# An encoder layer with unnormalised x tiles and the token norm applied at the projections' outputs

## The chip, the cores and the metric

The kernel runs on one core of a Trainium2 chip. The metric is the device time of one execution in microseconds, as the median of several runs. Engines are named as in the profile: PE (TensorE, with PEld for its weight loads), DVE (VectorE), ACT (ScalarE), POOL (GpSimd) and SP (the queue that issues nearly all DMAs).

## The reference

One hybrid encoder layer is applied to 768 tokens (512 of a prompt, 256 of a sample) of width 2048, in float32:

```
h = rms_norm(x, norm_g)                     # x / sqrt(mean(x^2)) * gain, a factor for each token
proj = h @ w_in                             # 2048 x 8224
attn = dilated_attention(aq, ak, av) * silu(ag)        # 8 heads x 128, three windows merged
q, k, v = silu(short_conv(dq, dk, dv))                 # centred, 5 taps, each channel for itself
dn = rms_norm(delta_rule_fwd + delta_rule_bwd) * silu(dg)   # gated DeltaNet, 8 heads, two directions
y = rms_norm(x + concat(attn, dn) @ w_out, final_gain)
```

The norm of the input is a factor for each token (over x's 2048 channels) times a gain for each channel. The projections are linear, so the token's factor may stand before or behind them.

## The kernel before, in words

Activations lie with channels on partitions: x comes as 16 tiles of 128 channels by 768 tokens. Every projection gives a tile of 128 output channels by 768 tokens in two PSUM banks (512 and 256 columns). Float32 accuracy comes from splitting each operand into a rounded high part and a rest (`w_split` L319, `x_split` L425) and adding three products: high by high, high by low, low by high (`kstep` L335). A high part is a cast on ScalarE, a low part a subtraction on VectorE (on GpSimd in some single tiles).

An order for all engines is written out while the program is built. A `Driver` (L68) runs the TensorE program as the main line and a clock of costs for each engine; between matmuls it takes up to three steps of side tasks, smallest priority number first. A task that yields `AHEAD` (2.0) goes on 2 us before its own work is expected to end. Each engine and each DMA queue then runs its instructions in the order in which they were written out.

The stages, in order:

1. As x tiles land, `arrivals` (L433) makes their split parts with the channel gain but without the token factor, and sums squares. The first call of `project_two` (L588, called at L1588) projects two DeltaNet gates from them, two output tiles at a time, and the 32 columns of decay and beta inputs; `raw_gate_post` (L881) multiplies their outputs by rB, the token factor on all partitions, which `start_rms` (L909) has by about 58 us.
2. A second `project_two` (L1592) does two more gates in the same way. Beside it `norm` (L748) goes through the 16 tiles as soon as the second projection has used each: VectorE multiplies the x tile by gain and rB in place, ScalarE casts the new high part over the old one, VectorE subtracts for the low part. For eight of the tiles the right halves are stored to DRAM (bD, L763), because they are overwritten later.
3. A third `project_two` (L1593, "std") makes q and k of attention head 0 from the normalised parts; it waits for each tile.
4. Ten pairs of weight tiles (v, gates of attention, last gates) are projected by a seven-product scheme for 2 x 2 blocks instead of eight (`pair_products` L662, table `PRODUCTS` L64): each pair in two halves (input tiles 0 to 7 and 8 to 15), each half seven products of 12 matmuls of 384 columns in banks X, Y and Z. `evacuate` (L695) combines the banks. The right operands T1 to T4 are sums of quarters of x. `block_sums` (L767) makes them, once for all pairs: eight calls, each with four differences (T1f, T2f, T3f, T4f) and four split results. T2's parts are written over the right half of an x tile's parts, once the third projection has used it (`reached["std"] > a`, L781). T3's two subtractions run on GpSimd, the other six on VectorE. `normalise` (L814) runs the norm and then the eight sums, one after the other. `restore` (L822) brings the right halves back from bD after the last pair.
5. 24 convolution tiles and the rest of attention's q and k, one tile at a time (`project` L632). `conv_post` (L833) copies a tile out of PSUM into the buffer cin and adds five taps: for q and k on VectorE, for v (tile 16 and on) with a ScalarE multiply into ctmp and a GpSimd add. DeltaNet's work (`prep`, `merge`, `chain`, `head_out`) and later attention (`scores`, `attend`) run as side tasks. Attention's heads alternate between two sets of buffers (`SETS`, L1408), whose V is loaded into cin or ctmp.
6. The output projection in two parts (DeltaNet's channels, then attention's), L1756 to L1798, beside the end of attention; then the final norm.

Of the kernel before, what the change touches and what calls it, by code (L numbers as in the profile page):

```python
# [6 lines left out]
F32 = mybir.dt.float32  # L7
# [250 lines left out]
def encoder_kernel(tc, x, xT, wt, wab, wo, convw, gain, dngain, fgain, alog, dtb, cst, tabs, y):  # L258
# [43 lines left out]
    with (  # L302
# [59 lines left out]
        set_pool(ap, dict({f"t{i}": (3 * KB, 1) for i in range(24)}, f768=(3 * KB, 3), half=(HALF, 3), rB=(T, 1), m=(5 * P, 1)))  # L362
        sums3 = [ap.tile([P, HALF], F32, name=f"sum{i}") for i in range(3)]

        if True:
# [51 lines left out]
            rB = st("rB", (T,), "rB")  # L417
# [277 lines left out]
            def evacuate(x, pr):  # L695
# [42 lines left out]
                if pr in (2, 3, 7, 4):  # L738
                    yield 0
                    x["n"][side] += 1  # L740
                    if ph and x["n"][side] == 2:
                        kind, h = x["kind"][side]
                        spawn(put_out(kind, h, x["out"][side]), -4)


            normal = set()

            def norm():  # L748

                for k in range(NK + 1):  # L750
                    if k < NK:
                        yield from wait(lambda: reached["raw"] > k)
                        xn = xstage[k]
                        V.scalar_tensor_tensor(out=xn, in0=xn, scalar=g_in[:, k:k + 1], in1=rB, op0=ALU.mult, op1=ALU.mult)
                        xtiles(k, "n")
                        A.copy(xh[k], xn)
                    if k:
                        p = k - 1
                        V.tensor_tensor(out=xl[p], in0=xstage[p], in1=xh[p].bitcast(F32), op=ALU.subtract)
                        normal.add(p)  # L760
                        if p % 8 < 4:

                            for t, d in zip((xh[p], xl[p]), bD[4 * (p // 8) + p % 4]):  # L763
                                SY.dma_start(d, t[:, HALF:].bitcast(F32))
                    yield AHEAD

            def block_sums(ph, i):  # L767
# [4 lines left out]
                t, d = {}, {}  # L772

# [22 lines left out]
                yield from diff("T3", xb[:, hi], xa[:, hi], G)  # L796
# [9 lines left out]
                low("T3", G)  # L806
# [7 lines left out]
            def normalise():  # L814
                yield from wait(lambda: "rms" in flags)
                yield from norm()
# [16 lines left out]
            def conv_post(ctile, dst, room, done):  # L833

                def conv(acc):
# [5 lines left out]
                    for j in range(1, 5):  # L841
                        if ctile >= 16:
                            ctmp = Z["ctmp"]
                            A.mul(ctmp, cin[:, j:j + w], cw[:, j:j + 1])
                            G.tensor_tensor(out=acc, in0=acc, in1=ctmp, op=ALU.add)
                            yield "early"
                        else:
                            V.scalar_tensor_tensor(out=acc, in0=cin[:, j:j + w], scalar=cw[:, j:j + 1], in1=acc,
                                                   op0=ALU.mult, op1=ALU.add)
                            yield "bulk"  # L850
# [10 lines left out]
                def post(ps):  # L861
                    yield from get("cin", "cacc")
                    for h in (0, 1):
                        o = (2, TP + 6)[h]
                        A.copy(Z["cin"][:, o:o + width[h]], ps[h][:, :width[h]])
# [5 lines left out]
            def spill_post(kind, h):  # L871

                def post(ps):
                    yield from get("f768")
                    t = f768(f"{kind}{h}")
                    A.copy(t[:, parts[0]], ps[0][:, :TP])
                    V.tensor_copy(t[:, parts[1]], ps[1][:, :TS])
# [133 lines left out]
            def conv_tiles():  # L1011
                Z["cin"] = st("cin", (T + 8,), "cin")
                Z["ctmp"] = st("ctmp", (T + 4,), "ctmp")
# [370 lines left out]
            def halves(h, what):  # L1384
# [16 lines left out]
                else:  # L1401
# [7 lines left out]
                    dict(vT="ctmp", V=("oacc", "DN"), tab="PB", g="PBT", s=("D0", "X0")))  # L1409
# [91 lines left out]
            def put_out(kind, h, t):  # L1501

                if kind in "gd":
# [335 lines left out]
```

## Time and profile before

| | |
|---|---|
| median of 3 runs (lowest to highest) | 1695.9 us (1695.44 to 1698.59) |
| the profiled execution: time, span | 1694.39 us, 1692.7 us |
| busy, share of the span | PE 94%, PEld 83%, DVE 53%, ACT 50%, POOL 19% |
| mean granted TensorE clock | 0.98 |
| PE's busy tenths in 40 slices of 42.3 us | 7994999999999999999999999999999889897995 |
| DVE's | 6689777767545453455435355544346545433332 |

A slice's digit is its busy share in tenths, 9 for 90% or more. A group of instructions is a line with its operation, the tile it writes and those it reads (buffer numbers left out); as most instructions go through one helper, L204 or L286 stands for nearly all, and the tile's name tells them apart: xst is an x tile, xh_n and xl_n its normalised parts, raw, hip and lop weight parts, st a loaded weight quarter, S its sums, mmr, mm, mmX, mmY, mmZ PSUM banks, sum and out what `evacuate` writes, cacc the convolution's sum, av and V attention's V, T1f a difference and T1s its split result. A wait is the idle time of an engine ahead of an instruction, and the row names what ended it.

### The profile page before, as it was taken

How to read it: one execution, taken by the hardware profiler on the slowest of the kernel's cores; microseconds unless marked ns; L12 is line 12 of the kernel's file. 1: busy time of each engine (PE TensorE's matmuls, PEld its weight loads, DVE VectorE, ACT ScalarE, POOL GpSimd, SP SyncE). 2: the span in 40 equal slices, each digit the busy share in tenths (PEclk: the TensorE clock that was granted, in tenths of full speed). 3: DMA queues.
4: the chain of work that ended last, by engine and by line, in shares of the span. 5: the costliest groups of instructions: out<-in, count | busy, mean ns of one | idle time of the engine just before them, and what ended most of it. 6: DMA issues, size and time to landing. Idle time of an engine off the chain costs nothing. (4 is left out here: it accounts for less than half of the span.)

```text
span 1692.7 us, 30222 instructions
## 1 busy us (share of the span) xinstructions
PE 1599.3 (94%) x11675; PEld 1411.9 (83%) x11675; DVE 896.6 (53%) x1903; ACT 852.2 (50%) x1896; POOL 316.2 (19%) x281
## 2 busy tenths in 40 slices
PE   7994999999999999999999999999999889897995
PEld 6884999999988898888898888888887777775774
DVE  6689777767545453455435355544346545433332
ACT  6554333343456665656575655665365444432322
POOL 0003000000125231424132323332100111101220
PEclk9997999999999999999999999999999999998998
DMA  6241232232523222232223122223344554346457
GB/s 241 86 139 44 79 108 94 94 108 93 199 75 94 70 82 82 79 103 77 80 75 106 61 79 79 90 74 100 107 158 161 179 178 157 113 138 214 151 170 273
DMA packets 135263, 198.50 MB, mean 117 GB/s; under 512 B 49392, under 2 KB 60240, under 8 KB 135120
## 3 DMA queue, kind: packets, MB, share of 16 engines
q1 hardware_dynamic: 133968, 193.43, 35.3%
q10 hardware_dynamic: 1152, 3.15, 0.5%
q8 instruction: 92, 1.51, 0.4%
q14 instruction: 51, 0.42, 0.1%
HBM read 150.08 MB, written 46.45 MB: 116 GB/s over the span
## 5 line engine op out<-in xcount | busy, mean ns | idle before, releaser
L286 PE MATMUL mm<-xh_n,lop 128*128 128x512 f32 (+1 forms) x1152 | 306.4, 347 | 0.0
L286 PE MATMUL mm<-xl_n,hip 128*128 128x512 f32 (+1 forms) x1152 | 306.0, 347 | 0.0
L286 PE MATMUL mm<-xh_n,hip 128*128 128x512 f32 (+1 forms) x1152 | 304.3, 345 | 0.0
L204 ACT CAST hip<-st 128x512 fp32r<-128x512 f32 x244 | 150.8, 619 | 228.1 <-PE mm L286 90.5
L204 DVE TENSOR_TENSOR lop<-st,hip 128x512 fp32r<-128x512 f32 x172 | 126.2, 734 | 236.0 <-ACT hip L204 214.4
L204 POOL TENSOR_TENSOR lop<-st,hip 128x512 fp32r<-128x512 f32 x72 | 96.6, 1342 | 620.2 <-ACT hip L204 571.2
L286 PEld LDWEIGHTS mm<-xh_n,hip 128*128 128x128 f32 x1152 | 176.2, 189 | 22.4
L286 PEld LDWEIGHTS mm<-xl_n,hip 128*128 128x128 f32 x1152 | 176.5, 189 | 21.6
L286 PEld LDWEIGHTS mm<-xh_n,lop 128*128 128x128 f32 x1152 | 176.4, 189 | 21.6
L204 ACT ACTIVATE s<-s,m 128x512 f32<-128x512 f32 (+1 forms) x96 | 61.9, 649 | 103.6 <-DVE m L204 103.3
L286 PE MATMUL mmo<-oh,xh_m 128*128 128x512 f32 x192 | 80.4, 419 | 8.6 <-ACT oh L204 6.8
L286 PE MATMUL mmo<-oh,mh 128*128 128x512 f32 x192 | 76.9, 400 | 11.7 <-ACT mh L204 10.9
L286 PE MATMUL mmo<-ol,xh_m 128*128 128x512 f32 x192 | 78.2, 407 | 3.2 <-POOL ol L204 2.2
L204 POOL TENSOR_TENSOR cacc<-cacc,ctmp 128x772 f32<-128x772 f32 x32 | 59.1, 1846 | 116.6 <-ACT ctmp L204 116.5
L204 DVE SCALAR_TENSOR_TENSOR cacc<-cin,cw,cacc 128x772 f32<-128x772 f32 x64 | 71.0, 1109 | 18.4 <-ACT cacc L204 17.5
L286 PE MATMUL mmo<-ol,mh 128*128 128x512 f32 x192 | 76.7, 400 | 0.5 <-DVE ol L204 0.5
L286 PE MATMUL mmo<-oh,xl_m 128*128 128x512 f32 x192 | 77.0, 401 | 0.0
L286 PE MATMUL mmo<-oh,ml 128*128 128x512 f32 x192 | 76.4, 398 | 0.0
L286 PE MATMUL mmX<-xh_n,hip 128*128 128x384 f32 x160 | 54.3, 340 | 18.5 <-ACT sum L204 18.0
L286 PE MATMUL mmr<-xh_x,raw 128*128 128x512 f32 (+1 forms) x256 | 60.1, 346 | 10.5 <-ACT xh_x L204 10.5
L204 ACT ACTIVATE z<-c,rho 128x128 f32<-128x128 f32 x96 | 35.1, 366 | 65.0 <-PE c L286 64.8
L204 DVE TENSOR_TENSOR ol<-st,oh 128x512 fp32r<-128x512 f32 x52 | 42.2, 843 | 36.5 <-ACT oh L204 36.4
(267 smaller groups left out, 3495.2 us busy)
## 6 DMA issues: line engine op xcount, KB each, us to landing
st<-in_wt SPq DMA_DIRECT2D x256, 256.0 KB
st<-in_wo SPq DMA_DIRECT2D x64, 256.0 KB
dec<-gcD SPq DMA_DIRECT2D x24, 256.0 KB
res<-in_x SPq DMA_DIRECT2D x24, 256.0 KB
yD<-res SPq DMA_DIRECT2D x24, 256.0 KB
res<-yD SPq DMA_DIRECT2D x24, 256.0 KB
out_y<-row SPq DMA_DIRECT2D x12, 512.0 KB
xst<-in_xT SPq DMA_DIRECT2D x15, 384.0 KB
```

The costliest lines, as they stand in the source:

```text
L204: r = f(*a, **k)
L286: r = PE.matmul(out, lhsT, rhs, start=start, stop=stop, skip_group_check=more)
```

## The change

The token factor is not multiplied into x any more. `norm` is gone; the split parts of the first projections serve all later ones. Where a projected tile leaves PSUM, it is multiplied by rB: in `conv_post` and `spill_post` in place of a copy (on VectorE, some of it from ScalarE), and in the pairs by a multiply in place ahead of the store (`put_out`, raw). `block_sums` multiplies its two x tiles by the channel gain on ScalarE, stores the right halves to bD itself, and makes T3 on VectorE. The generator of the sums doesn't wait for the token factor. The taps of v's convolution run on VectorE as those of q and k, without ctmp, and both attention sets load V into cin. A test for three free banks stands ahead of each part of the output.

```diff
-            def norm():
...
-                        V.scalar_tensor_tensor(out=xn, in0=xn, scalar=g_in[:, k:k + 1], in1=rB, op0=ALU.mult, op1=ALU.mult)
-                        xtiles(k, "n")
-                        A.copy(xh[k], xn)
...
-                        V.tensor_tensor(out=xl[p], in0=xstage[p], in1=xh[p].bitcast(F32), op=ALU.subtract)
...
             def block_sums(ph, i):
...
+                for v, dst in zip((xh[a], xl[a]), bD[4 * ph + i]):
+                    SY.dma_start(dst, v[:, HALF:].bitcast(F32))
+                for k in (a, a + 4):
+                    A.mul(xstage[k], xstage[k], g_in[:, k:k + 1])
+                yield AHEAD
...
-                yield from diff("T3", xb[:, hi], xa[:, hi], G)
+                yield from diff("T3", xb[:, hi], xa[:, hi])
...
-                low("T3", G)
+                low("T3")
...
-            def normalise():
-                yield from wait(lambda: "rms" in flags)
-                yield from norm()
+            def all_sums():
                 for ph in (0, 1):
                     for i in range(4):
                         yield from block_sums(ph, i)
...
-                        if ctile >= 16:
-                            ctmp = Z["ctmp"]
-                            A.mul(ctmp, cin[:, j:j + w], cw[:, j:j + 1])
-                            G.tensor_tensor(out=acc, in0=acc, in1=ctmp, op=ALU.add)
-                            yield "early"
...
+                        V.scalar_tensor_tensor(out=acc, in0=cin[:, j:j + w], scalar=cw[:, j:j + 1], in1=acc,
+                                               op0=ALU.mult, op1=ALU.add)
+                        yield "bulk"
...
-                        A.copy(Z["cin"][:, o:o + width[h]], ps[h][:, :width[h]])
+                        V.tensor_tensor(out=Z["cin"][:, o:o + width[h]], in0=ps[h][:, :width[h]], in1=rB[:, parts[h]], op=ALU.mult)
...
-                    A.copy(t[:, parts[0]], ps[0][:, :TP])
-                    V.tensor_copy(t[:, parts[1]], ps[1][:, :TS])
+                    for i in (0, 1):
+                        V.tensor_tensor(out=t[:, parts[i]], in0=ps[i][:, :width[i]], in1=rB[:, parts[i]], op=ALU.mult)
...
-                    dict(vT="ctmp", V=("oacc", "DN"), tab="PB", g="PBT", s=("D0", "X0")))
+                    dict(vT="cin", V=("oacc", "DN"), tab="PB", g="PBT", s=("D0", "X0")))
...
-            def put_out(kind, h, t):
+            def put_out(kind, h, t, raw=False):
+
+                if raw:
+                    V.tensor_tensor(out=t, in0=t, in1=rB, op=ALU.mult)
+                    yield 0
...
-            spawn(normalise(), -8)
+            spawn(all_sums(), -8)
...
-            project_two([p for _, p in first], lambda k: drv.until(lambda: k in normal), "std")
+            project_two([p for _, p in first], lambda k: None, "std")
...
                         group = 3
+                        drv.until(lambda: free("mm", group))
                         ps3 = [bank(f"o{part}_{t}") for t in range(group)]
```

## Rows read from the trace of the kernel before

**Rows 1.** Waits of TensorE from 90 to 180 us: engine, line, waited for: total, times, longest.

```profile
PE mmX L286 <- ACT sum L204: 18.0, 1, 18.0
PE mmZ L286 <- DVE sum L204: 4.4, 1, 4.4
PE mmY L286 <- DVE out L204: 2.5, 1, 2.5
```

**Rows 2.** Busy us in two stretches: stretch, length, PE, PEld, DVE, ACT, POOL, clock, DMA, GB/s.

```profile
100.70:130.30 29.60, 29.60 (x172) 25.89 (x170) 24.11 (x35) 15.20 (x28) 1.13 (x2) 1.00 0.39 134
130.30:174.70 44.40, 18.98 (x86) 18.05 (x86) 41.76 (x60) 18.47 (x37) 15.39 (x13) 0.73 0.12 42
```

**Rows 3.** Timeline of TensorE around the third projection and the first pair.

```profile
96.47 0.60 PE L286 MATMUL mmr<-xh_n,raw 128*128 128x512 f32 x2
...
130.82 0.45 PE L286 MATMUL mmX<-xh_n,hip 128*128 128x384 f32 x1 [0.48 <-ACT q L204]
...
151.68 0.52 PE L286 MATMUL mmX<-xl_n,hip 128*128 128x384 f32 x1
152.00 0.52 PE L286 MATMUL mmX<-xh_n,lop 128*128 128x384 f32 x1
...
174.68 0.33 PE L286 MATMUL mmX<-xh_n,hip 128*128 128x384 f32 x1
...
176.75 0.34 PE L286 MATMUL mmY<-xh_n,hip 128*128 128x384 f32 x1
...
187.52 0.59 PE L286 MATMUL mmY<-T4s,hip 128*128 128x384 f32 x2 [0.20 <-DVE out L204]
```

**Rows 4.** Operations by tile (first and last start) and by group (mean ns), VectorE and ScalarE.

```profile
L204 DVE SCALAR_TENSOR_TENSOR xst<-xst,g_in,rB x16: 1005/1012/1014, 68.4 to 121.3; 128x768 f32<-128x768 f32 x16
...
L204 DVE TENSOR_TENSOR ab<-ab,rB x2: 404/539/674, 61.5 to 62.1; 64x512 f32<-64x512 f32 x1, 64x256 f32<-64x256 f32 x1
...
L204 DVE TENSOR_TENSOR T1f<-xst x8: 541/547/1344, 125.5 to 170.2; 128x384 f32<-128x384 f32 x8
...
L204 DVE TENSOR_TENSOR T2f<-xst,T1f x8: 557/558/559, 126.1 to 170.8; 128x384 f32<-128x384 f32 x8
...
L204 DVE TENSOR_TENSOR xl_n<-xst,xh_n 128x768 fp32r<-128x768 f32 x16 | 15.2, 950 | 0.0
...
L204 DVE TENSOR_TENSOR raw<-st,raw 128x256 fp32r<-128x256 f32 x29 | 11.6, 433 | 14.4 <-ACT raw L204 13.6 <-DMA gD<-gated 0.8
...
L204 DVE TENSOR_TENSOR lop<-S,hip 128x512 fp32r<-128x512 f32 x6 | 4.1, 686 | 1.2 <-ACT hip L204 1.2
...
L204 DVE TENSOR_TENSOR out<-mmY,sum 128x384 f32<-128x384 f32 x40 | 22.0, 549 | 0.0
...
L204 ACT ACTIVATE xh_x<-xst,g_in 128x768 fp32r<-128x768 f32 x15 | 13.9, 926 | 0.0
```

**Rows 5.** Stores of the x halves on SP, a wait of SP, and one store's landing.

```profile
L248 SPq DMA_DIRECT2D bD<-xh_n x8: 327/424/529, 71.4 to 113.0; - x8
...
SPq L248 <- DVE lop L204: 38.1, 6, 24.0
...
1520.58 2.27 DMA mixD<-ag
```

**Rows 6.** Busy us in the pairs and in the convolution stage (columns as in rows 2).

```profile
205.00:430.00 225.00, 225.00 (x1293) 223.19 (x1292) 161.81 (x279) 83.15 (x140) 0.00 (x0) 1.00 0.29 101
455.00:1255.00 800.00, 794.45 (x7436) 699.19 (x7435) 374.19 (x925) 480.08 (x1189) 239.71 (x216) 1.00 0.29 87
```

**Rows 7.** VectorE's convolution taps.

```profile
L204 DVE SCALAR_TENSOR_TENSOR cacc<-cin,cw,cacc 128x772 f32<-128x772 f32 x64 | 71.0, 1109 | 18.4 <-ACT cacc L204 17.5
```

**Rows 8.** Timeline of SP, VectorE and TensorE where the first two attention heads load V.

```profile
1244.02 0.42 SPq L248 DMA_DIRECT2D av<-vD  x1
...
1247.70 0.42 DVE L204 TENSOR_TENSOR V<-av,V 128x256 fp32r<-128x256 f32 x1 [0.51 <-ACT V L204]
...
1275.50 0.60 PE L291 MATMUL av<-ident,av 128*128 128x128 f32 x4
```

More of the change, by code (lines that the diff above doesn't have):

```diff
@@ L361, in encoder_kernel @@
         ap = ap_cm.__enter__()
-        set_pool(ap, dict({f"t{i}": (3 * KB, 1) for i in range(24)}, f768=(3 * KB, 3), half=(HALF, 3), rB=(T, 1), m=(5 * P, 1)))
+        set_pool(ap, dict({f"t{i}": (3 * KB, 1) for i in range(24)}, f768=(3 * KB, 3), half=(HALF, 3), m=(5 * P, 1)))
         sums3 = [ap.tile([P, HALF], F32, name=f"sum{i}") for i in range(3)]
@@ L416, in encoder_kernel @@
             xacc = st("t23", (T,), "xacc")
-            rB = st("rB", (T,), "rB")
+            rB = keep([T], "rB")
             xstage, xdone, raw, sq = {}, set(), set(), [0]
@@ L742, in evacuate @@
                         kind, h = x["kind"][side]
-                        spawn(put_out(kind, h, x["out"][side]), -4)
-            normal = set()
-            def norm():
[L750 to L753, printed above, removed]
-                        V.scalar_tensor_tensor(out=xn, in0=xn, scalar=g_in[:, k:k + 1], in1=rB, op0=ALU.mult, op1=ALU.mult)
-                        xtiles(k, "n")
-                        A.copy(xh[k], xn)
-                    if k:
-                        p = k - 1
-                        V.tensor_tensor(out=xl[p], in0=xstage[p], in1=xh[p].bitcast(F32), op=ALU.subtract)
[L760 to L765, printed above, removed]
+                        spawn(put_out(kind, h, x["out"][side], True), -4)
             def block_sums(ph, i):
@@ L841, in conv @@
                     for j in range(1, 5):
-                        if ctile >= 16:
-                            ctmp = Z["ctmp"]
-                            A.mul(ctmp, cin[:, j:j + w], cw[:, j:j + 1])
-                            G.tensor_tensor(out=acc, in0=acc, in1=ctmp, op=ALU.add)
-                            yield "early"
[L847 to L850, printed above, removed]
+                        V.scalar_tensor_tensor(out=acc, in0=cin[:, j:j + w], scalar=cw[:, j:j + 1], in1=acc,
+                                               op0=ALU.mult, op1=ALU.add)
+                        yield "bulk"
                     give("cin")
@@ L1012, in conv_tiles @@
                 Z["cin"] = st("cin", (T + 8,), "cin")
-                Z["ctmp"] = st("ctmp", (T + 4,), "ctmp")
                 for a, b in ((0, 2), (514, 518), (774, 776)):
@@ L1655, in open_heads @@
                     PB=(1056, 1), PBT=(4 * KB, 1), dec=(2 * KB, 3), ktok=(3 * KB, 2), vtok=(3 * KB, 2), oacc=(3 * KB, 1),
-                    cin=(T + 8, 1), ctmp=(T + 4, 1), cacc=(T + 4, 1), tmp=(112, 1), T3=(384, 1), LM=(384, 1),
+                    cin=(T + 8, 1), cacc=(T + 4, 1), tmp=(112, 1), T3=(384, 1), LM=(384, 1),
                     D0=(512, 1), X0=(512, 1)))
```

## The prediction

> **What bounds the kernel now.** I read the page's slices first, then TensorE's waits, then one stretch by engine, then VectorE's groups. In the slices (the table of the profile) TensorE is at nine tenths or more nearly everywhere, with one deep notch, the fourth slice. Its waits there are named: 18.0 us for a ScalarE copy of a product's bank, 4.4 and 2.5 us for VectorE, 24.9 us together [rows 1]. All three lie in the first half-pair, seven products of 12 matmuls. One undisturbed product takes 174.68 to 176.75, 2.07 us [rows 3], so a half takes 14.5; this one lasts from 130.3 to 174.7, 44.4 us [rows 2]. The place costs 29.9 us: the waits, and the lower clock behind them (0.73 as mean of the half [rows 2]). ScalarE is no cause: it is busy 18.5 of the 44.4 us, VectorE 41.8, 94% [rows 2]. The copy stands in ScalarE's queue behind casts that wait for VectorE. So VectorE is the bound, with the norm's work (68.4 to 122 us) and then the eight block sums, whose first differences run from 125.5 to 170.2 us [rows 4].
>
> **What the change removes.** From VectorE the norm's 16 multiplies of 1.01 us and 16 subtractions of 0.95, 31.4 us [rows 4]. They lie where TensorE did not wait; their going is worth only what the sums can start earlier. On ScalarE 16 casts go, and 16 multiplies by the gain come, one for each x tile, of 0.93 us [rows 4].
>
> **When the sums can start.** They don't start with x: the generator is still spawned behind the first projection, the sums run one after the other, and each T2 is written over the right half of an x tile that the third projection (q0, k0) still reads. So the first sum stops at its T2 until that projection is through k-steps 0 and 1. It starts at 96.47 us and ends at 130.3 [rows 2, 3], 2.1 us a k-step: the gate opens at 100.7 us. The later gates open faster than VectorE can use them.
>
> **VectorE's bill from 100.7 us.** The second half needs the T2 of four more sums at its second product. Up to there VectorE must do:
> - of the sums, 59 operations of 0.558 us (the T2 difference [rows 4]): five left of the first sum, eight in each of the next six, six of the last: 32.9 us. GpSimd's T3 pair is now among them;
> - 11 weight pieces of 0.433 us left in the third projection, 4.8; two gates by rB, 0.95 each (as the subtraction of that size), 1.9;
> - pair weights: nine low parts and seven sums of quarters, 16 by 0.686, 11.0;
> - five evacuations of the first half by 0.549, 2.7; q0's and k0's, each in parts of 512 and 256, 0.674 and 0.404 (nearest row: the same multiply by rB on 64 partitions [rows 4]), 2.2.
>
> That is 55.5 us; at VectorE's 94% of before, 59.0: the second product of the second half can begin at 159.7 us. Before, it began at 176.75 [rows 3]. Without any wait it would begin at 130.3 + 14.5 + 2.1 = 146.9, so a wait of some 13 us stays there in place of the three. Gain 17.0 us.
>
> Against that: **(a)** the clock. The remaining wait is nearly as long as the 18.0 us one, after which matmuls started 0.32 us apart [rows 3] instead of 2.07/12 = 0.17. Between nothing and a whole product, 12 by 0.15 = 1.8 us; I take 1.5. **(b)** The first pair already waited 0.48 us for q0's evacuation [rows 3]; two engines shared it, now VectorE does both parts, plus 0.5. **(c)** T2 may be written only when the store of that half x tile to DRAM has read it. The 16 stores, 192 KB each, were issued from 71 us to behind 113, SP spending 0.42 us on one [rows 5]; 14 of them now come within the sums. Nothing shows their landing; the nearest row is a 384 KB store of 2.27 us [rows 5]. Bounds: nothing (1.85 us of multiplies and the differences come between) to 7 by 2.27, 15.9 us. SP works in order, past weight loads of which one waited 24.0 us for VectorE [rows 5]; a store behind such a load comes late, and with T2's cast ScalarE's next weight casts, which VectorE and then TensorE need. I take 2 us, near the lower end, since the multiplies cover most of a landing. Together 4.0; gain 13.0 us.
>
> **A rule against the change.** GpSimd's T3 pair cost VectorE already: the first difference took 0.541 us alone and up to 1.344 beside it [rows 4]. Two such holds in a sum are 1.6 us, two more VectorE operations 1.1, so moving T3 costs nothing. The Trainium skill ("Perfetto Trace Analysis", Optimizing Scalar/DVE Operations) advises to take work off a saturated VectorE, to ScalarE or even GpSimd, though it adds that the port which GpSimd and VectorE share may spoil the latter. By the advice alone the move would cost 8 by 1.1, 8.9 us, and the gain would be 4.1; the 1.344 us row bears out the caveat, and none of the 8.9 enters the sum.
>
> **Where the rest is hidden.** Ten pairs get 20 multiplies by rB of 0.95 us, 19 us. From 205 to 430 us TensorE is busy all 225 us and VectorE 162, 72% [rows 6]; it becomes 80%, and the 63 spare us cover it: a multiply comes behind a finished half, where the next product's weights are made. In the convolution stage (455 to 1255) VectorE is busy 374 of 800 us [rows 6] and gets 32 taps of 1.11 us [rows 7], 24 evacuations of 0.674 + 0.404, and 0.674 more for each of 14 spills: 35.5 + 25.9 + 9.4 = 71 us, to 56%. ScalarE loses 32 multiplies, GpSimd 32 adds. TensorE is busy 794 of the 800, so I cost it at nothing; without that cover a bank freed later than a projection takes (16 us) would stop it. Both attention sets now take V from one buffer. Head 0 freed its own at 1248.1, head 1's load was issued at 1244.02, 4.1 us too early, but read from 1275.5 on [rows 8]: covered. The new test for three free banks ahead of the output is one of order, not a wait in an engine's queue; TensorE had to have those banks evacuated anyway.
>
> **Sum.** The profiled execution took 1694.39 us, 1.7 more than its span. 1694.4 - 13.0 = 1681.4; the median of the runs lies 1.5 above that execution: 1682.9, **1683 us**.
>
> **Rivals.**
> - *All of it goes* (10%): the sums are ahead whenever asked; 29.9 us less, 1666. For it: VectorE is idle 5.5 of the 29.6 us to 130.3 [rows 2], and norm work leaves it. Against: 59 operations that cannot begin before the gate.
> - *The stores take it back* (20%): T2's casts wait for the stores, up to the 15.9 us of (c). From half of that, 1689, to all of it, 1697; half the chance lies within 0.2% and half below. For: SP's 24.0 us wait in just this stretch. Against: VectorE has low parts to do meanwhile.
> - *Slower* (12%): the multiplies by rB reach TensorE in the pairs. A half's last product needs the bank of the last product but one evacuated, so VectorE has one product's 2.07 us; TensorE waited 0.20 us there already, at 187.52 [rows 3]. If all 20 stood in the way, 19 us: 1702. It decides from the 14th of the 20 on (13.0 / 0.95). Against: 28% of VectorE is idle there, and TensorE has no gap in 225 us.
> - *My forecast* (58%): 1677 to 1689: VectorE at 100% (156.2 us) with half of the deductions, a gain of 18.5; or at 85% (166.0 us) with all of them, 6.7.
>
> **Numbers.** 0.2% (3.4 us) is about what a measurement of this kernel can tell from no change. Faster by more: 58 + 10 + 10 = 78%; within: 10%; slower: 12%. The range, 1670 to 1695, holds all of the fourth, most of the second (18 of its 20) and some of the first (4 of 10), and leaves out the third: 80%.
>
> **What would show it.** Right: the 18.0 us wait for ScalarE gone; one wait of 10 to 15 us at the second product of the second half, ended by VectorE or T2's cast; the first T1 difference near 70 us but the first T2 cast at 100 to 101; the last T1 difference by 157 instead of 170; differences of 0.56 us throughout; no gap of TensorE from 205 to 430. Wrong: ScalarE idle ahead of T2's casts because of a DMA; waits for "out" or "sum" in every pair; a first and a second half of 14.5 us each (the first rival); T2 casts ahead of 100 us.

## The result, and the profile after

| | before | after |
|---|---|---|
| median of 4 runs (lowest to highest) | 1695.67 us (1694.73 to 1698.59) | 1656.24 us (1655.21 to 1661.15) |
| profiled execution: time, span | 1694.39, 1692.7 us | 1661.15, 1659.4 us |

The ratio is 0.977, 95% interval 0.9748 to 0.9793: 39.4 us less, where 13 were forecast. The profiled execution of after lies 4.9 us above its median, so its span differs from before's by only 33.3 us; within the traces those 33.3 are to be explained.

The page of the changed kernel (busy shares, then busy tenths in 40 slices of 41.5 us):

```profile
PE 1597.8 (96%) x11675; PEld 1411.5 (85%) x11675; DVE 934.0 (56%) x2003; ACT 799.6 (48%) x1800; POOL 237.2 (14%) x233
...
PE   7998999999999999999999999999999889999995
...
DVE  6558877778445554556555555665355555444332
```

The notch in the fourth slice has gone from four tenths to eight. But there is a second difference: towards the end TensorE has two slices at eight tenths, where before had "889897". That stage was not part of the forecast.

TensorE's waits from 90 to 180 us, changed kernel:

```profile
PE mmX L286 <- ACT sum L204: 3.5, 1, 3.5
PE mmY L286 <- DVE out L204: 2.7, 2, 2.2
PE mmY L286 <- DVE xl_x L204: 0.5, 1, 0.5
```

These are 6.7 us in place of 24.9 [rows 1]. The windows (columns as in rows 2) of the third projection's end, the first half-pair, the pairs and the convolution stage:

```profile
100.70:130.20 29.50, 29.50 (x169) 25.54 (x169) 21.42 (x47) 18.71 (x36) 0.00 (x0) 1.00 0.38 125
130.20:155.10 24.90, 19.23 (x86) 18.49 (x85) 21.36 (x41) 13.31 (x24) 0.00 (x0) 0.80 0.33 113
205.00:430.00 225.00, 223.11 (x1272) 221.18 (x1272) 170.00 (x285) 82.00 (x139) 0.00 (x0) 0.99 0.32 108
455.00:1255.00 800.00, 792.64 (x7439) 697.81 (x7438) 431.07 (x1038) 437.49 (x1116) 174.39 (x176) 1.00 0.29 88
```

The first half takes 24.9 us instead of 44.4 [rows 2], still not the undisturbed 14.5. TensorE's timeline around it:

```profile
130.19 0.34 PE L286 MATMUL mmX<-xh_x,hip 128*128 128x384 f32 x1
...
151.58 0.58 PE L286 MATMUL mmY<-T4s,hip 128*128 128x384 f32 x2 [2.17 <-DVE out L204]
...
155.11 0.52 PE L286 MATMUL mmX<-xh_x,hip 128*128 128x384 f32 x1
...
157.41 0.33 PE L286 MATMUL mmY<-xh_x,hip 128*128 128x384 f32 x1
...
160.15 0.44 PE L286 MATMUL mmY<-xl_x,hip 128*128 128x384 f32 x1 [0.54 <-DVE xl_x L204]
...
171.88 0.33 PE L286 MATMUL mmX<-xh_x,hip 128*128 128x384 f32 x1
```

The second product of the second half starts at 157.41 (before 176.75 [rows 3]) and the second pair at 171.88, where before's starts at 189.68:

```profile
189.68 0.33 PE L286 MATMUL mmX<-xh_n,hip 128*128 128x384 f32 x1
```

So 17.8 us are gained there. At the end of the pairs (the first matmul into mm) 14.2 are left, 439.0 against 453.2. These are the rows of that end, first start behind the comma: before, the changed kernel, and a_evcv, a version below.

```profile
L286 PE MATMUL mm<-xh_n,hip x1152: 274/339/580, 453.2 to 1240.9; 128*128 128x512 f32 x192
...
L286 PE MATMUL mm<-xh_x,hip x1152: 274/391/628, 439.0 to 1234.4; 128*128 128x512 f32 x192
...
L286 PE MATMUL mm<-xh_x,hip x1152: 274/342/590, 436.9 to 1220.0; 128*128 128x512 f32 x192
```

a_evcv is edited behind the pairs only; up to there its engines and SP run the changed kernel's instructions in the same order, yet its pairs end 2.1 us earlier. Five versions of before (b_vdve, b_rest, b_hop, b_hop13, b_side4) that are alike in the same way end theirs at 454.2 to 455.3. Each of these ends is one execution, and a difference of some 2 us between two of them shows nothing.

The later milestones, by tile: DeltaNet's last state updates (c), and the output's first part (xh_m) and second part (mh), first and last start. Before:

```profile
L286 PE MATMUL c<-z,in x192: 270/273/377, 595.3 to 1238.3; 128*128 128x128 f32 x192
...
L286 PE MATMUL mmo<-oh,xh_m x192: 387/393/777, 1291.7 to 1524.7; 128*128 128x512 f32 x192
...
L286 PE MATMUL mmo<-oh,mh x192: 390/393/794, 1536.4 to 1673.9; 128*128 128x512 f32 x192
```

After:

```profile
L286 PE MATMUL c<-z,in x192: 270/273/377, 580.5 to 1216.9; 128*128 128x128 f32 x192
...
L286 PE MATMUL mmo<-oh,xh_m x192: 387/389/797, 1297.5 to 1501.0; 128*128 128x512 f32 x192
...
L286 PE MATMUL mmo<-oh,mh x192: 390/393/628, 1501.7 to 1640.8; 128*128 128x512 f32 x192
```

DeltaNet ends 21.4 us earlier, the second output part starts 34.7 us earlier. So the 33.3 us between the two profiles divide into 14.2 up to the end of the pairs, 7.2 from there to DeltaNet's end (785.1 to 777.9), 13.3 from there to the second output part (298.1 to 284.8), and 1.4 given back behind it. TensorE's waits between DeltaNet's end and the second output part, before:

```profile
PE mmo L286 <- ACT mh L204: 10.9, 1, 10.9
PE mmo L286 <- ACT oh L204: 6.8, 5, 2.7
PE S L286 <- ACT khi L204: 6.3, 2, 3.3
```

and after:

```profile
PE mmo L286 <- DVE q L204: 4.1, 1, 4.1
PE S L286 <- POOL qklo L204: 3.4, 3, 1.5
PE av L291 <- DVE V L204: 3.0, 1, 3.0
PE S L286 <- ACT khi L204: 2.6, 2, 2.0
```

Before, the first part of the output was done (1525) before attention's last result had reached the second part, and TensorE waited 10.9 us at the handover. After, the first part still runs when that result comes, and the wait is not among the largest.

### The profile page after: what moved, and what is told of

Its sections match the earlier page's. It is cut to its first block, busy times and chain, and to the rows that moved or that the text cites. A ratio compares the mean times of both kernels' runs of the same rounds, so it can differ in the third digit from the quotient of the medians.

```text
span 1659.4 us, 30160 instructions
## 1 busy us (share of the span) xinstructions
PE 1597.8 (96%) x11675; PEld 1411.5 (85%) x11675; DVE 934.0 (56%) x2003; ACT 799.6 (48%) x1800; POOL 237.2 (14%) x233
## 4 chain that ended last, share of the span: by engine, by line
PE 80%; DMA 6%; DVE 5%; issue 4%; ACT 3%; POOL 1%; SPq 1%; ACTq 0%; DVEq 0%; POOLq 0%
PE mm L286 36%; PE mmo L286 8%; PE mmY L286 7%; PE mmr L286 7%; PE c L286 5%; PE mmX L286 5%; PE mmZ L286 5%; PE m L286 2%; DMA out_y<-row 2%; DMA st<-in_wo 1%; PE kk L286 1%; PE o L286 1%; DMA ak<-kD 1%; PE S L286 1%; DMA res<-in_x 1%
## 5 line engine op out<-in xcount | busy, mean ns | idle before, releaser
L286 PE MATMUL mm<-xl_x,hip 128*128 128x512 f32 (+1 forms) x1152 | 307.2, 348 | 0.0
L286 PE MATMUL mm<-xh_x,lop 128*128 128x512 f32 (+1 forms) x1152 | 305.5, 346 | 0.0
L286 PE MATMUL mm<-xh_x,hip 128*128 128x512 f32 (+1 forms) x1152 | 304.5, 345 | 0.0
L286 PEld LDWEIGHTS mm<-xh_x,hip 128*128 128x128 f32 x1152 | 176.5, 189 | 22.8
L286 PEld LDWEIGHTS mm<-xh_x,lop 128*128 128x128 f32 x1152 | 176.6, 189 | 21.7
L286 PEld LDWEIGHTS mm<-xl_x,hip 128*128 128x128 f32 x1152 | 176.4, 189 | 21.2
L286 PE MATMUL mmr<-xh_x,raw 128*128 128x512 f32 (+1 forms) x512 | 118.5, 345 | 11.3 <-ACT xh_x L204 9.6
L204 DVE SCALAR_TENSOR_TENSOR cacc<-cin,cw,cacc 128x772 f32<-128x772 f32 x96 | 107.4, 1119 | 23.4 <-ACT cacc L204 22.0
L286 PEld LDWEIGHTS mmr<-xh_x,raw 128*128 128x128 f32 x512 | 79.7, 191 | 25.3 <-ACT xh_x L204 9.9
L286 PE MATMUL mmr<-xl_x,raw 128*128 128x512 f32 (+1 forms) x256 | 67.0, 343 | 0.4 <-DVE xl_x L204 0.4
```

The costliest lines, as they stand in the source:

```text
L204: r = f(*a, **k)
L286: r = PE.matmul(out, lhsT, rhs, start=start, stop=stop, skip_group_check=more)
```

## The experiments

Two questions were put: whether the head of the pairs works as the forecast says, and where the gain behind the pairs comes from. All versions are listed once; the stage lengths are from their profiled executions ("pairs": first matmul into mm; "to DeltaNet": from there to the last c<-z,in; "to part 2": from there to the first mmo<-oh,mh). "Evac" is the engine that takes the convolution and spill tiles out of PSUM.

| version | evac | median us | ratio to before, interval | pairs | to DeltaNet | to part 2 |
|---|---|---|---|---|---|---|
| before | ACT | 1695.67 | 1 | 453.2 | 785.1 | 298.1 |
| b_hop | ACT | 1696.58 | 1.0001 (0.9986 to 1.0015) | 454.7 | 781.3 | 299.0 |
| b_hop13 | ACT | 1702.50 | 1.004 (1.0019 to 1.0061) | 455.0 | 795.5 | 293.7 |
| b_side4 | ACT | 1676.78 | 0.9892 (0.9863 to 0.9921) | 455.3 | 774.5 | 292.7 |
| b_vdve | ACT | 1687.65 | 0.9954 (0.9939 to 0.9968) | 454.2 | 786.9 | 294.2 |
| b_rest | ACT | 1691.40 | 0.9972 (0.996 to 0.9984) | 455.2 | 787.3 | 292.1 |
| b_all | DVE | 1677.44 | 0.9902 (0.9874 to 0.9931) | 456.4 | 779.9 | 282.5 |
| b_all4 | DVE | 1671.83 | 0.9869 (0.9841 to 0.9898) | 456.9 | 782.2 | 276.2 |
| after | DVE | 1656.24 | 0.977 (0.9748 to 0.9793) | 439.0 | 777.9 | 284.8 |
| a_early | DVE | 1655.29 | 0.9759 (0.9735 to 0.9783) | 434.7 | 776.5 | 284.0 |
| a_t3gp | DVE | 1662.20 | 0.9801 (0.9771 to 0.9831) | 442.0 | 776.1 | 285.5 |
| a_st | DVE | 1657.41 | 0.9773 (0.9737 to 0.9809) | 438.1 | 776.1 | 286.6 |
| a_noraw | DVE | 1655.09 | 0.9759 (0.9725 to 0.9792) | 435.4 | 775.7 | 282.4 |
| a_hop | DVE | 1678.39 | 0.9895 (0.9874 to 0.9915) | 435.7 | 797.2 | 287.0 |
| a_hop13 | DVE | 1687.17 | 0.9953 (0.9918 to 0.9988) | 438.6 | 805.9 | 286.0 |
| a_side4 | DVE | 1651.39 | 0.9742 (0.9714 to 0.9771) | 438.2 | 780.7 | 276.7 |
| a_noev | ACT | 1671.51 | 0.9867 (0.9826 to 0.9908) | 436.8 | 783.3 | 291.1 |
| a_evcv | both | 1669.48 | 0.9843 (0.9814 to 0.9872) | 436.9 | 785.2 | 290.1 |
| a_evsp | both | 1674.09 | 0.987 (0.9842 to 0.9899) | 435.9 | 783.3 | 297.3 |
| a_early4 | DVE | 1648.20 | 0.973 (0.9701 to 0.9758) | 434.8 | 779.5 | 274.0 |

### The head of the pairs

**a_early**: the differences of T1, T3 and T4 go ahead of the gate, T2's is kept in the x tile, and a task of its own splits it when the gate opens.

```diff
-                yield from diff("T2", xb[:, hi], t["T1"])
-                yield from high("T2")
+                V.tensor_tensor(out=xa[:, lo], in0=xb[:, hi], in1=t["T1"], op=ALU.subtract)
+                spawn(second(), -9)
```

> The changed kernel, with each block sum split: T1, T3 and T4 are made as soon as there is room, the T2 difference is kept in the x tile itself, and only T2's cast and low part stay behind the third projection. Theory D (what is left of the head's loss is VectorE's work behind the gate, 59 operations at 0.47 us from start to start): about 20 operations go ahead of the gate, the pairs end 7 to 10 us earlier than in the changed kernel (439.0 us), at 429 to 432. Theory E (the loss left is ScalarE's order, or the clock): within 3 us of 439. The total time can differ by the order of the last stage (20 us between two orders of the same work so far), so the pairs' end decides, not the total.

The pairs end 4.3 us earlier than in the profile of after and 2.2 earlier than in a_evcv: less than theory D asked, and by the first figure more than theory E. The median fell by 0.9, and its interval overlaps that of after. From the first pair's start to the second's it takes 39.4 us (130.98 to 170.33), where the changed kernel takes 41.7 (130.19 to 171.88). The waits of the first half are still there (1.4, 2.6 and 3.6 us, 7.6 in all against 6.7), but TensorE's clock from 130.2 to 160 is 0.94 instead of 0.83, and VectorE is busy 22.6 of these 29.8 us instead of 26.2. So the gate is one cause of what is left at the head, worth some 2 us. Waits for single results make up the rest; why these come late was not tried.

**a_t3gp**: T3's two subtractions back on GpSimd.

```diff
-                yield from diff("T3", xb[:, hi], xa[:, hi])
+                yield from diff("T3", xb[:, hi], xa[:, hi], G)
...
-                low("T3")
+                low("T3", G)
```

> The changed kernel with T3's two subtractions back on GpSimd. My prediction held that T3's move costs nothing, because VectorE is held up beside GpSimd. If so, the pairs end at 436 to 442 us (439.0 in the changed kernel) and VectorE's differences show up to 1.3 us again. If GpSimd's work were free, VectorE would have 14 operations of 0.47 us less behind the gate: 6 to 7 us earlier, 432.

The pairs end 3.0 us later than in the profile of after and 5.1 later than in a_evcv, at the upper edge of what was expected; the median is 6.0 higher, with intervals that overlap. Its first differences by tile, against those of the changed kernel below:

```profile
L204 DVE TENSOR_TENSOR T1f<-xst x8: 541/547/1355, 65.9 to 160.2; 128x384 f32<-128x384 f32 x8
```

```profile
L204 DVE TENSOR_TENSOR T1f<-xst x8: 545/550/559, 62.9 to 157.1; 128x384 f32<-128x384 f32 x8
```

The long one runs beside GpSimd's subtraction:

```profile
65.33 1.52 POOL L204 TENSOR_TENSOR T3f<-xst,xst 128x384 f32<-128x384 f32 x1 [64.40 <-DMA st<-in_wt]
...
65.91 1.35 DVE L204 TENSOR_TENSOR T1f<-xst 128x384 f32<-128x384 f32 x1
```

With GpSimd at T3 a first difference takes up to 1.355 us again; without it none takes over 0.559. Moving T3 to the engine that was full gained some 3 to 5 us at this place, by one execution of a_t3gp.

**a_st**: all 16 stores of the x halves are issued at once, ahead of the first sum.

```diff
-                for v, dst in zip((xh[a], xl[a]), bD[4 * ph + i]):
-                    SY.dma_start(dst, v[:, HALF:].bitcast(F32))
...
+                for p in range(8):
+                    for v, dst in zip((xh[8 * (p // 4) + p % 4], xl[8 * (p // 4) + p % 4]), bD[p]):
+                        SY.dma_start(dst, v[:, HALF:].bitcast(F32))
```

> The changed kernel with the sixteen stores of the x halves issued together, right behind the first projection, instead of two at the start of each sum. If T2's casts wait for the stores (my deduction of 2 us, up to 15.9), the pairs end 2 to 8 us earlier than 439.0 us. If they are covered, within 1.5 us of it.

The pairs end 0.9 us earlier, within what two executions differ by, and the median is the same within its interval. No cost of the stores shows.

**a_noraw**: no multiply by rB of the pairs' outputs.

```diff
-                if raw:
-                    V.tensor_tensor(out=t, in0=t, in1=rB, op=ALU.mult)
-                    yield 0
```

> The changed kernel without the multiply by rB of the pairs' outputs (v, gates of attention and the last gates stay without the token factor). In the changed kernel the pairs took 267.1 us from the second to the end, with one wait of 1.9 us for a bank behind a store, and the lower clock after it. If the multiplies cause that by making the store late behind the reloads of the x halves, it goes and the pairs end 3 to 4 us earlier, near 435.5. If it is only the reloads, the end stays at 438 to 440.

The pairs end 3.6 us earlier than in the profile of after. The changed kernel has one wait late in the pairs that this version lacks. SP's, VectorE's and TensorE's timeline of the changed kernel there:

```profile
408.83 0.33 SPq L248 DMA_DIRECT2D xh_x<-bD  x1
...
412.05 0.43 SPq L248 DMA_DIRECT2D xl_x<-bD  x1
...
413.00 0.91 SPq L248 DMA_DIRECT2D gD<-out  x2
...
419.86 0.56 DVE L204 TENSOR_TENSOR out<-mmY,sum 128x384 f32<-128x384 f32 x1 [2.01 <-DMA gD<-out]
...
420.57 0.59 PE L286 MATMUL mmY<-T4s,hip 128*128 128x384 f32 x2 [1.89 <-DVE out L204]
```

The stores of the last pair but one (413.00) stand on SP behind the eight reloads of x halves that the last pair begins with (408.83 to 412.05). The last pair's output needed their buffer: VectorE waited 2.01 us for the store, TensorE 1.89 for VectorE, and the clock fell to 0.91 between 420 and 440 us. In a_noraw, where one of the stores stands ahead of the reloads (407.99), TensorE has no wait from 400 to 440 us.

But a_evcv has none there either, with every multiply in place and the same order on SP and VectorE:

```profile
419.35 0.56 DVE L204 TENSOR_TENSOR out<-mmY,sum 128x384 f32<-128x384 f32 x1 [0.21 <-DMA gD<-out]
```

VectorE waits 0.21 us for the same store, and the clock from 420 to 440 us is 1.00. From the second pair to the end of the pairs before takes 263.5 us, a_noraw 263.4, a_evcv 263.7 and after 267.1. So the pairs lose from 0.2 to 3.6 us with the multiplies in place, as the execution has it; the profile of after is the longest of all versions here.

### Behind the pairs: single parts in the kernel before

**b_vdve**: only v's taps on VectorE.

```diff
-                            A.mul(ctmp, cin[:, j:j + w], cw[:, j:j + 1])
-                            G.tensor_tensor(out=acc, in0=acc, in1=ctmp, op=ALU.add)
+                            V.scalar_tensor_tensor(out=acc, in0=cin[:, j:j + w], scalar=cw[:, j:j + 1], in1=acc,
+                                                   op0=ALU.mult, op1=ALU.add)
```

> The kernel before, with the taps of v's convolution on VectorE alone. Of the 33 us between the two profiles only 18.8 us of TensorE's idle time went from the stretch of the first pair; 16 us went from the last stage, where attention runs beside the output. Theory A (the taps: ScalarE and GpSimd are freed, so DeltaNet and attention finish earlier against the main line): 10 to 18 us faster, and the 10.9 us wait at the change of the output's parts gone. Theory B (the plan is written out by a model of costs, and any edit shifts the last stage by chance): within 8 us on either side, wait of another length. Theory C (the norm's change alone carries it): within 3 us of the kernel before.

**b_rest**: this, with V shared in cin and the test for three banks.

```diff
-                    dict(vT="ctmp", V=("oacc", "DN"), tab="PB", g="PBT", s=("D0", "X0")))
+                    dict(vT="cin", V=("oacc", "DN"), tab="PB", g="PBT", s=("D0", "X0")))
...
+                        drv.until(lambda: free("mm", group))
```

> The kernel before with all parts of the change that don't touch the norm: v's taps on VectorE, one buffer for both attention sets' V, the test for three free banks. Theory A: as the taps alone, 10 to 18 us faster. Theory B: another value within 8 us. Theory C: within 3 us of the kernel before. If the test for banks or the shared buffer matter, this differs from the taps alone by more than 3 us.

The taps alone bring 8.6 us against the 1696.28 us of before measured beside them (24 runs), the three parts together 4.9; the two intervals overlap. Theory A fails: the gain is under its 10 us, and the handover's wait for mh stays in both, 11.1 and 10.8 us. Theory C fails too (more than 3 us). Theory B's span holds both (the taps' gain is 7.8 us by the ratio), which does not yet show that the order is the cause. The taps on GpSimd were not tried in the changed kernel, which has no buffer ctmp.

### The written-out order

The order of all engines is planned with a few constants. These runs change one constant and no work.

**b_hop**, **a_hop** (HOP, the plan's cost of passing a result to another engine, 0.12 to 0.14), **b_hop13**, **a_hop13** (0.13):

```diff
-HOP = 0.12
+HOP = 0.14
```

> The kernel before with one constant of the planner's model changed (0.12 to 0.14 us between engines) and no instruction added or removed: only the order written out can differ. Theory B: the time moves by 3 to 15 us, in the first pair and in the last stage. Theories A and C: within 3 us.

> The changed kernel with the same constant changed. Theory B: 3 to 15 us from the changed kernel's 1656, most likely slower, since 1656 would be a lucky order. Theories A and C: 1653 to 1660.

> The kernel before with HOP 0.13 instead of 0.12, so another written-out order and no other work. From the end of the last pair to the start of the second part of the output all versions of before took 1079 to 1084 us so far, and five of six of the changed kernel 1058 to 1063 (the sixth, a_hop, 1084). Theory F, the 20 us belong to the change's work (the pairs end early and VectorE's tasks are fewer steps): 1079 to 1085 again, time 1690 to 1700. Theory B, they hang on the written-out order alone: this order may come out at either length, 1058 to 1063 (time near 1675) or 1079 to 1085.

> The changed kernel with HOP 0.13. Pairs end at 436 to 442 us under both theories. Theory F: last pair to second output part 1058 to 1063 us, time 1652 to 1662. Theory B: either that or 1079 to 1085, the latter with a time of 1673 to 1680.

**b_side4**, **a_side4**: up to four steps of side tasks between two matmuls.

```diff
-SIDE_MAX = 3
+SIDE_MAX = 4
```

> The kernel before with up to four steps of side tasks between two matmuls instead of three: attention can be written out further ahead of the main line. Theory F: last pair to second output part 1079 to 1085 us, time 1690 to 1700. Theory B: either that or about 1060 us, the latter with a time near 1675 if the first half-pair is as before (pairs end near 453).

> The changed kernel with up to four steps of side tasks between two matmuls. Pairs end at 436 to 442 us. Theory F: last pair to second output part 1058 to 1063 us, time 1652 to 1662. Theory B: either that or 1079 to 1085, the latter with a time of 1673 to 1680.

The same work takes 1676.8 to 1702.5 us in before and 1651.4 to 1687.2 us in the changed kernel. In a_hop the pairs end even earlier than in after (435.7), yet it takes 22 us longer: DeltaNet ends 797.2 us behind the pairs instead of 777.9, and the stretch behind it has nearly its old length (287.0 against 284.8). So theory B holds in this form: the stretch to DeltaNet's end depends on the order written out, 774 to 796 us in before and 778 to 806 in the changed kernel. Its numbers were often missed: b_hop moved by 0.3 us, a_hop by more than 15, and in b_hop13 and a_hop13 the way from the pairs' end to the second output part took 1089 and 1092 us, more than either theory had. b_side4 gets half of the change's gain with none of its work.

Two versions under the same constants, side by side, say what the whole change is worth there (the last three columns are differences of the table above):

| constants | before, us | changed, us | gain, us | pairs end earlier by, us | change of "to DeltaNet" | change of "to part 2" |
|---|---|---|---|---|---|---|
| as they were | 1695.67 | 1656.24 | 39.4 | 14.2 | -7.2 | -13.3 |
| HOP 0.14 | 1696.58 | 1678.39 | 18.2 | 19.0 | +15.9 | -12.0 |
| HOP 0.13 | 1702.50 | 1687.17 | 15.3 | 16.4 | +10.4 | -7.7 |
| four steps | 1676.78 | 1651.39 | 25.4 | 17.1 | +6.2 | -16.0 |

The head's gain and the shorter last column are there under all four. The stretch to DeltaNet's end is shorter in the changed kernel only under the constants as they were, and longer under the other three. The 39.4 us are the largest of the four gains, so part of them is luck of the order.

The last column is 292 to 299 in the six versions of before so far, 277 to 287 in the changed kernel under these constants. The next runs looked for the part behind it.

### The evacuations

**b_all** is b_rest with the evacuations on VectorE (as copies), **b_all4** the same with four steps; **a_noev** is the changed kernel with the evacuations as before.

```diff
-                        A.copy(Z["cin"][:, o:o + width[h]], ps[h][:, :width[h]])
+                        V.tensor_copy(Z["cin"][:, o:o + width[h]], ps[h][:, :width[h]])
...
-                    A.copy(t[:, parts[0]], ps[0][:, :TP])
-                    V.tensor_copy(t[:, parts[1]], ps[1][:, :TS])
+                    for i in (0, 1):
+                        V.tensor_copy(t[:, parts[i]], ps[i][:, :width[i]])
```

> The kernel before with every part of the change but the norm's: v's taps on VectorE, one buffer for V, the test for three banks, and the evacuations of the convolution and spill tiles on VectorE (as copies, since the token factor is already in x). Pairs end at 453 to 456 us in any case. Theory E, ScalarE's relief from the evacuations shortens attention: from DeltaNet's end to the second part of the output 284 to 287 us instead of 292 to 299, time near 1680. Theory N, it comes only with the norm's change: 292 to 299 again, time 1688 to 1696.

> As b_all, with up to four steps of side tasks between two matmuls. Pairs end at 453 to 456 us. Theory E: DeltaNet's end to the second output part 277 to 287 us, time 1662 to 1670. Theory N: 290 to 294 as in b_side4 (292.7), time 1673 to 1680. If this comes near 1656, nearly the whole measured gain is to be had without the change of the norm.

> The changed kernel with the evacuations of the convolution and spill tiles as before (ScalarE and VectorE copies); these tiles lack the token factor. Pairs end at 437 to 440 us. Theory E: DeltaNet's end to the second output part back at 292 to 299 us, time 1664 to 1675. Theory N: 282 to 287, time 1652 to 1662 (up to 20 more if DeltaNet ends late, more than 785 us behind the pairs).

The move of the evacuations turns b_rest's 1691.4 into 1677.4, and taking it out of the changed kernel turns 1656.2 into 1671.5: 14 and 15 us by the medians (12 and 16 by the ratios, since before itself, measured beside b_all and a_noev, was 2 to 3 us lower), with intervals that don't meet. The last column follows it, 282.5 against 292.1 and 284.8 against 291.1, within 2 us of what theory E of these runs asked. So the move of the evacuations shortens the end in these orders; whether by ScalarE's relief, as the theory has it, is another question. b_all's rows by tile, with before's head and the changed kernel's tail:

```profile
L286 PE MATMUL c<-z,in x192: 270/273/377, 598.0 to 1236.3; 128*128 128x128 f32 x192
...
L286 PE MATMUL mmo<-oh,xh_m x192: 387/389/793, 1317.0 to 1518.2; 128*128 128x512 f32 x192
...
L286 PE MATMUL mmo<-oh,mh x192: 387/393/500, 1518.8 to 1657.6; 128*128 128x512 f32 x192
```

And a_noev's waits from DeltaNet's end to the second part, with before's tail behind the changed head:

```profile
PE mmo L286 <- ACT mh L204: 10.6, 1, 10.6
PE mmo L286 <- ACT oh L204: 6.2, 3, 3.3
PE S L286 <- POOL qklo L204: 5.1, 4, 1.5
```

The wait of 10.6 us at the handover is back. With four steps all the parts behind the norm are worth less: b_side4 to b_all4 is 1676.8 to 1671.8, 5.0 us, with intervals that overlap. The last column falls there by 16.5 us, and the stretch to DeltaNet's end grows by 7.7.

**a_evcv** and **a_evsp** put back one group each: the 48 evacuations of convolution tiles, and those of q and k. The latter are 16 tiles and not the 12 that were expected: 12 in the convolution stage, q0 and k0 at 128 to 133 us, and two at 1270 to 1277 us.

```diff
-                        V.tensor_tensor(out=Z["cin"][:, o:o + width[h]], in0=ps[h][:, :width[h]], in1=rB[:, parts[h]], op=ALU.mult)
+                        A.copy(Z["cin"][:, o:o + width[h]], ps[h][:, :width[h]])
```

```diff
-                    for i in (0, 1):
-                        V.tensor_tensor(out=t[:, parts[i]], in0=ps[i][:, :width[i]], in1=rB[:, parts[i]], op=ALU.mult)
+                    A.copy(t[:, parts[0]], ps[0][:, :TP])
+                    V.tensor_copy(t[:, parts[1]], ps[1][:, :TS])
```

> The changed kernel with the 48 evacuations of the convolution tiles back on ScalarE (23 us of ScalarE, by its copies of 0.58 and 0.38 us in a_noev); these tiles lack the token factor. If these decide: 1668 to 1675 us, DeltaNet's end to the second output part 289 us or more. If attention's spilled tiles decide, or the written-out order alone does in a way that any edit shifts: as the changed kernel, 1652 to 1662 us and 282 to 287 us.

> The changed kernel with the evacuations of the 12 spilled q and k tiles as before (512 columns on ScalarE, 7 us in all, 256 on VectorE); these tiles lack the token factor. If the convolution tiles decide: 1652 to 1662 us, DeltaNet's end to the second output part 282 to 287 us. If the spilled tiles decide: 1668 to 1675 us and 289 us or more.

Each of the two alone loses 13.2 and 17.9 us, about as much as both together (15.3), though they hold 23 and 9 us of ScalarE's time. By what was expected, each would be the one that decides, which can't be true of both. The loss does not grow with the work put back. That speaks against a plain relief of ScalarE and for the order that the plan writes out; it was not settled, since this planner writes another order for every edit of the work.

**a_early4** is a_early with four steps:

> The early sums of a_early and up to four steps of side tasks, computing all that the reference asks. If the pieces add: pairs end at 434 to 436 us (as a_early), the rest as in a_side4, so 1651.4 - 4 = 1647 us. If the order of the last stage changes again with the head: 1650 to 1680.

1648.2 us, the lowest of all; its interval overlaps that of a_side4. Against a_side4 the pairs end 3.4 us earlier, the median is 3.2 lower and the ratio by 2.0 us. That agrees with pieces that add, but doesn't show it.

## Why the prediction was wrong

The direction was right, and so was most of the head; the size was not. The step that failed is the part on where the rest is hidden: it costed the new work of the convolution stage "at nothing", asked only what it could harm, and took everything behind the pairs to keep its length, though the planner writes another order for it. Between the two profiles 19.1 of the 33.3 us came from behind the pairs: 7.2 up to DeltaNet's end and 13.3 from there to the second output part, less 1.4. Under the two other values of HOP the change gained 18.2 and 15.3 us with 19.0 and 16.4 at the head, so there the rest, one stretch longer and one shorter, did come to about nothing.

- **The norm's part.** b_all has every part but this one; the changed kernel takes 21.2 us less (1677.4 to 1656.2), and with four steps 20.4 less (1671.8 to 1651.4); by the ratios 22.4 and 21.5. Its worth stayed the same under the two constants tried; b_all was not run under the other values of HOP. At the end of the pairs it is 17.4 and 18.7 us. The forecast's head had the right mechanism: 17.0 before deductions, and the deductions of 4.0 do not show.
- **The bill.** VectorE was through the bill's 59 operations at 160.1 us, where the forecast has 159.7, but by two errors that cancel, and that is luck: it was busy 47.7 us from 100.7 on where the bill has 55.5, and 80% of the time, not 94%. The bill priced an operation by its row's duration; one behind the other they start closer together (below). It also had two gates by rB that were done before 100.7. The second product of the second half came at 157.41, ahead of the end of the bill: it takes the T2s one by one and waited only 0.54 us for the last (160.15). The wait was not one of 13 us at that product either: a first half of 24.9 us held it up, with waits of 3.5 and 2.2 us and a clock of 0.80.
- **The gate.** The first cast of a T2 ran at 100.86 us, within the forecast's 100 to 101; the first difference of T1 was at 62.9 (forecast 70), the last at 157.1 (forecast 157). a_early, which goes round the gate, has the second pair 2.3 us sooner behind the first.
- **Deductions.** (a) The clock: matmuls 0.32 us apart reach only to the second half's second matmul, 155.43; the second half took 16.8 us (155.11 to 171.88) against 14.5 undisturbed. (b) The first pair did not wait for q0's evacuation. In b_all, where VectorE is still full of the norm, it did, 2.1 us. (c) ScalarE waited once for a store ahead of a T2's cast, 1.52 us at 151.62, which the forecast had as a sign of being wrong; with all stores issued ahead (a_st) the pairs end within the spread of the executions. So 17.8 us were gained at the second pair, against 17.0 before deductions.
- **T3.** Costed at nothing; it gained 3 to 5 us at the end of the pairs. The advice of the Trainium skill ("Perfetto Trace Analysis", Optimizing Scalar/DVE Operations) to take work off a saturated VectorE would have lost this; its caveat, that the two share a port and such a move might not help, fits the 1.355 us row.
- **Multiplies in the pairs.** VectorE's share rose to 76% (170.0 of 225 us; forecast 80%). The *slower* rival's multiplies reached TensorE in the pairs at most once, and not by VectorE's time but by a wait for a store behind the reloads: 0.2 (a_evcv) to 3.6 us (after) of the 19 that the rival asked for. The forecast's "no gap" from 205 to 430 us failed in the profile of after.
- **The convolution stage.** VectorE got 57 us more (431 against 374 of 800; forecast 71), and TensorE stayed at 792.6 of 800. Nothing was lost in this order, as forecast; under the three other constants the stretch to DeltaNet's end grew by 6.2 to 15.9 us. What the forecast did not ask is what ScalarE's 43 us less (480 to 437) and another order would give. In this order the parts behind the norm brought 18.9 us before it (1696.3 to b_all's 1677.4; 16.6 by the ratio): 4.9 for b_rest's three and 14.0 for the evacuations.
- **The rivals.** The first (1666) had TensorE's whole notch gone; 10.4 us of the first half and 2.3 of the second are still there. That the stores take it back does not show (17.8 us were gained at the second pair). None of the rivals had a gain outside the head, so the range ended at 1670.

What stays open: how much of the 18.9 us is the parts' own. With three steps of side tasks they bring 18.9, with four 5.0, and a constant of the plan moves the same kernel by up to 31 us (a_hop13 against after). A run that changes a part and keeps the rest of the written order was not made.

## What to carry to other kernels

Where a program's order is written out by a planner, every edit is two edits: the work and the order. Before a gain far from the edit is credited to the edit, run both kernels under a few neighbouring constants of the plan; what keeps its size under all of them can be credited to the edit, and the best constant may be worth half as much as the edit or more (here 19 us with none of the work changed, and 39, 18, 15 and 25 us for the edit under four settings). One profile is one execution: before a few microseconds of a stage are explained, look at versions that are written out alike up to there. Price a moved stream of operations by the distance of their starts, not by their durations, and ask of every move of work between engines what it does to the stages behind, even where the engines' busy shares are half.

## What the runs showed of the hardware

The rows of independent VectorE operations overlap. VectorE's timeline of the changed kernel, and below it that of before, where T2f stands right behind the T1f that it reads:

```profile
129.10 0.55 DVE L204 TENSOR_TENSOR T1f<-xst 128x384 f32<-128x384 f32 x1
129.56 0.55 DVE L204 TENSOR_TENSOR T3f<-xst,xst 128x384 f32<-128x384 f32 x1
130.03 0.55 DVE L204 TENSOR_TENSOR T2f<-xst,T1f 128x384 f32<-128x384 f32 x1
130.50 0.55 DVE L204 TENSOR_TENSOR T1s<-T1f,T1s 128x384 fp32r<-128x384 f32 x1
```

```profile
125.51 0.55 DVE L204 TENSOR_TENSOR T1f<-xst 128x384 f32<-128x384 f32 x1
126.09 0.56 DVE L204 TENSOR_TENSOR T2f<-xst,T1f 128x384 f32<-128x384 f32 x1
```

Each lasts 0.55 us, and the next starts 0.46 to 0.47 after it began; the T1f that T2f reads has ended by then. In before T2f starts 0.58 us after its T1f began. So T3f, set between the two, puts T2f back by only 0.35 us (0.93 against 0.58). For the 59 operations of the bill 0.47 us each would be 27.7 us instead of 32.9, an estimate.

The Trainium skill ("Vector Engine (DVE) Microarchitecture Reference", Measured stream behaviour on trn2) gives 1.04 ns a column and 75 ns an operation, an estimate of 475 ns for 384 columns; the trace agrees (0.47 us from start to start).

A subtraction of GpSimd beside VectorE made a VectorE difference of 384 columns last up to 1.355 us instead of 0.55, as in the kernel before [rows 4]. In a_t3gp the pairs ended at 442.0 us, in three executions of the changed kernel's order (after, a_evcv, a_side4) at 436.9 to 439.0: here the full engine lost more by two operations on the free one than by doing them itself.

The same store kept VectorE waiting 2.01 us in one execution and 0.21 in another (after and a_evcv), with the same order on the engines and on SP.
